# Attention logits on all 128 rows: query halves stacked, key halves written twice

## The chip, the cores and the metric

The kernel runs on one core of one Trainium2 chip. The time is device microseconds of one execution; the number for a kernel is the median of its runs. A core has engines that run side by side, each with a queue of its own: TensorE (PE; its weight loads are listed apart, as PEld), VectorE (DVE), ScalarE (ACT), GpSimd (POOL), and SyncE (SP), which starts transfers. TensorE writes its products to PSUM, eight banks of 128 partitions x 512 float32.

## The reference

One layer of a hybrid block on 512 tokens of width 1024, in float32: RMSNorm; one wide input projection; a gated linear attention branch; a forgetting attention branch (FoX); per-channel sigmoid gates that merge both; an output projection; a gated MLP with a short convolution; a last RMSNorm. The change touches FoX alone:

```python
for i in range(S // Q_BLOCK):                       # 4 blocks of 128 queries
    lo, hi = i * Q_BLOCK, (i + 1) * Q_BLOCK
    logits = jnp.einsum('bhqd,bhkd->bhqk', qh[:, :, lo:hi], kh[:, :, :hi]) * scale
    logits = logits + c[:, :, lo:hi, None] - c[:, :, None, :hi]
    p = softmax(where(mask, logits, -inf))
    outs.append(jnp.einsum('bhqk,bhkd->bhqd', p, vh[:, :, :hi]))
```

There are 8 heads (FH) of width 64 (FD). Query and key are RMS-normalised first.

## The kernel before, in words

TensorE multiplies in a float32 form (`F32R`) that keeps fewer bits. So each operand is split into a high half (a rounded copy, made by ACT) and a low half (what is left, made by DVE), and a product is high x high + high x low + low x high: three matmuls (`mm3`, L323, whose three lines 324 to 326 are most of the profile). Weights come in pieces of 128x1024, loaded by SP, split by ACT (L287) and DVE (L288) three pieces ahead of their use.

The attention loop (L1077) handles two heads, a "pair", at a time: heads 2p and 2p+1 lie on partitions 0-63 and 64-127 of the transposed query and key. For each of four pairs it goes through three groups of query blocks, (0,1), (2) and (3), so 12 steps.

- `prepare_k(pair)` (L936) transposes the pair's key on TensorE (four 128x128 blocks) into a PSUM bank, then ACT copies the high half `kh` (L942) and DVE subtracts the low half `kl` (L943), all 128 partitions at once. `prepare_q` (L947) does so for the query, with a scale per partition (L953, L954). Both kinds of tiles have two buffers.
- `logits(pair, qbs)` (L969): for each query block three products, (qh, kh), (ql, kh), (qh, kl), each once per head, with 64 rows of contraction per head (L979). Then for each head, on DVE, the logits minus their bias with the row maximum (L986), on ACT the exponential with its sum (L991), the reciprocal on DVE and the scaling on ACT (L993). The bias rows `cb` are loaded by SP and masked by POOL (L626 to L628).
- `transposed(h, qbs)` (L1003) transposes the probabilities, and splits them (L1029, L1030); `values(h, half)` (L1034) multiplies them with the value's halves, side by side in one 128-column operand (L1047, L1048).

The steps are software pipelined: in turn i the logits of step i, the transposes of step i-1, the values of step i-2. Between them TensorE works off a list, `work`, by `fill(n)`: n steps of it. Most of the list are gate products (`gate_tile`, L921: 8 steps of three 128x512 matmuls, then one DVE multiplication, L928, that frees the gate's PSUM bank); `prepare_k` and `prepare_q` are in it as steps of their own. The first fills of a turn are put behind the logits on TensorE's queue by hand (`tc.issue_after`, L1079). PSUM in this stage is four kinds of two banks: `mm` (gates, and the transposed query and key), `lg` (logits), `pt`, `po`.

Within these orders the framework's scheduler places the instructions of each engine when the kernel is built: a later instruction that is ready goes ahead of an earlier one that isn't.

Of the kernel before, what the change touches and what calls it, by code (L numbers as in the profile page):

```python
# [9 lines left out]
F32 = mybir.dt.float32  # L10
F32R = mybir.dt.float32r
BF16 = mybir.dt.bfloat16
I32 = mybir.dt.int32
AF = mybir.ActivationFunctionType
ALU = mybir.AluOpType
# [3 lines left out]
P = 128  # L19
T = 512  # L20
# [8 lines left out]
FH, FD = 8, 64  # L29
# [13 lines left out]
QSTEP = 4  # L43
# [41 lines left out]
def hybrid_kernel(ctx: ExitStack, tc, xT, xt, wp, wu, wd, wf, wn, pp, aw2, fing, out):  # L85
    nc = tc.nc
    mm = nc.tensor.matmul
# [16 lines left out]
    def bank(tag):  # L104
        return banks_of[tag].tile([P, 512], F32, tag=tag, name="ps_" + tag)
# [267 lines left out]
    for _ in range(NWARM):  # L373
        mm(  # L374
            warm, lhsT=nc.const_aps.tensor(1.0, (P, P), BF16), rhs=nc.const_aps.tensor(1.0, (P, T), BF16),
            start=True, stop=True,
# [10 lines left out]
    def col(c, rows=P):  # L387
        return ppt[:rows, c : c + 1]
# [5 lines left out]
        out=negm, in_=negm, pattern=[[-1, P]], base=0, channel_multiplier=1, compare_op=ALU.is_ge, fill=-1e30  # L394
# [5 lines left out]
        out=gmask, in_=gmask, pattern=[[1, P]], base=0, channel_multiplier=-1, compare_op=ALU.is_ge, fill=0.0  # L400
# [26 lines left out]
    work = []  # L427

    def fill(n=1 << 30):
        while n > 0 and work:  # L430
            try:
                next(work[0])
                n -= 1
            except StopIteration:
                work.pop(0)
# [75 lines left out]
    for k in range(KD):  # L511
        high = nc.scalar.activation(out=xh[k], in_=xrs[k], func=AF.Copy, scale=col(C_MIX + k))
        split_next()
        with tc.issue_after(first_copy[-1].ins):
            low = nc.vector.scalar_tensor_tensor(
                out=xl[k], in0=xrs[k], scalar=col(C_MIX + k), in1=xh[k].bitcast(F32),
                op0=ALU.mult, op1=ALU.subtract,
# [46 lines left out]
    gqs = cpool.tile([P, 1], F32, name="gqs")  # L564
    with tc.issue_after(low.ins):
        nc.vector.scalar_tensor_tensor(
            out=gqs, in0=col(C_QG), scalar=FD ** -0.5, in1=col(C_KG), op0=ALU.mult, op1=ALU.mult
# [27 lines left out]
    for j in range(2):  # L595
# [4 lines left out]
            out=mz[:, j, :], in0=pz, scalar1=col(C_AB + j), scalar2=0.0, op0=ALU.add, op1=ALU.min  # L600
# [11 lines left out]
        out=bz.rearrange("p a b -> p (a b)"), data0=rmask, data1=mz.rearrange("p a b -> p (a b)"),  # L612
# [4 lines left out]
        out=fm, data0=ones[:FH, 0:1].broadcast_to([FH, T]), data1=ft, initial=0.0, op0=ALU.mult, op1=ALU.add,  # L617
# [183 lines left out]
    for i in range(4):  # L801
        tag = ("ft", "fm", "sc2", "sc3")[i]
# [8 lines left out]
    for tt in range(NT):  # L811
        for j in range(2):
            t = slice(tt * P, (tt + 1) * P)
            c = slice((2 * (tt % 2) + j) * P, (2 * (tt % 2) + j + 1) * P)
            for par in range(2):
                r = slice(par * CH, (par + 1) * CH)
# [9 lines left out]
    def chunk_kv(c, j):  # L826
        i = 2 * (c // 2 % 2) + j
        return pkv[c // 4 * 2 + c % 2][:, i * GDV : (i + 1) * GDV]

    for tt in range(NT):  # L830
        for j in range(2):
            for par in range(2):
                for c in range(2 * tt, min(2 * tt + 2, NC - 1)):
                    r = slice(c % 2 * CH, (c % 2 + 1) * CH)
                    mm(
                        chunk_kv(c, j)[par * CH : (par + 1) * CH],
                        lhsT=kdt[r, tt, j, par * CH : (par + 1) * CH],
                        rhs=vg[r, tt, (2 * j + par) * GDV : (2 * j + par + 1) * GDV],
                        start=True, stop=True,
                    )  # L840
    for tt in range(NT):
        fill(2)
        for c in range(2 * tt, min(2 * tt + 2, NC - 1)):
            for j in range(2):
                if c == 0:
                    last_dve = nc.vector.tensor_copy(out=prev[:, j, 1, :], in_=chunk_kv(c, j))
                else:
                    last_dve = nc.vector.scalar_tensor_tensor(
                        out=prev[:, j, c + 1, :], in0=prev[:, j, c, :], scalar=dec[:, j * NC + c : j * NC + c + 1],
                        in1=chunk_kv(c, j), op0=ALU.mult, op1=ALU.add,  # L850
# [24 lines left out]
    for u in range(2):  # L875
        for par in range(2):
            for t2, j, c in quarters:
# [4 lines left out]
                    rhs=vg[:, 2 * u + t2, h * GDV : (h + 1) * GDV],  # L882
                    start=(t2 == j == 0), stop=False, skip_group_check=True,
                )
    for u in range(2):
        for t2, j, c in quarters:
            for par in range(2):
                r = slice(par * CH, (par + 1) * CH)
                for cp in range(2):
# [3 lines left out]
                        rhs=prev[r, j, ck, :], start=False, stop=True, skip_group_check=True,  # L893
                    )
    for u in range(2):
        for par in range(2):
            for t2, j, c in quarters:
                junk = gpool.tile([P, GDV], F32, tag="gjunk", name="gjunk", bufs=2)
                nc.scalar.activation(
                    out=junk, in_=obs[u][par][:, c], func=AF.Square, accum_out=gssq[:, u, par, t2, j : j + 1]  # L900
# [11 lines left out]
    fpool = es_f.enter_context(tc.tile_pool(name="fpool", bufs=1, reuse_waits="tile"))  # L912
# [8 lines left out]
    def gate_tile(z):  # L921
        ps = pmm()
        wh, wl = piece()
        for k in range(KD):
            c = slice(k * P, (k + 1) * P)
            mm3(ps, wh[:, c], wl[:, c], xh[k], xl[k], k == 0, k == KD - 1)
            yield
        nc.vector.tensor_mul(out=z, in0=ps, in1=rb)  # L928

    gates = [gate_tile(z) for z in zr + zg]  # L930


    psum(mm=2, lg=2, pt=2, po=2)
    qk, vs = {}, {}

    def prepare_k(pair):  # L936

        pk = bank("mm" if pair else "po")
        for tt in range(NT):
            nc.tensor.transpose(pk[:, tt * P : (tt + 1) * P], kf[:, tt, pair * P : (pair + 1) * P], ident)  # L940
        kh, kl = (fpool.tile([P, T], F32R, tag=tag, name=tag, bufs=2) for tag in ("kh", "kl"))
        nc.scalar.copy(out=kh, in_=pk)  # L942
        nc.vector.tensor_sub(out=kl, in0=pk, in1=kh.bitcast(F32))  # L943
        qk[pair] = [kh, kl]
        yield

    def prepare_q(pair):  # L947

        pq = bank("mm" if pair else "pt")
        for tt in range(NT):  # L950
            nc.tensor.transpose(pq[:, tt * P : (tt + 1) * P], qf[:, tt, pair * P : (pair + 1) * P], ident)
        qh, ql = (fpool.tile([P, T], F32R, tag=tag, name=tag, bufs=2) for tag in ("qh", "ql"))
        nc.scalar.activation(out=qh, in_=pq, func=AF.Copy, scale=gqs)  # L953
        nc.vector.scalar_tensor_tensor(  # L954
            out=ql, in0=pq, scalar=gqs, in1=qh.bitcast(F32), op0=ALU.mult, op1=ALU.subtract
        )
        qk[pair] += [qh, ql]
        yield

    def prepare_v(h):  # L960
# [7 lines left out]

    def logits(pair, qbs):  # L969

        kh, kl, qh, ql = qk[pair]
        rows = [slice(i * FD, (i + 1) * FD) for i in range(2)]
        lgs = [bank("lg") for _ in range(2)]
        for qb in qbs:
            n = (qb + 1) * P
            q = slice(qb * P, n)
            for j, (a, b) in enumerate(((qh, kh), (ql, kh), (qh, kl))):
                for lg, r in zip(lgs, rows):
                    last = mm(lg[:, place_of_q(qb)], lhsT=a[r, q], rhs=b[r, :n], start=(j == 0), stop=(j == 2))  # L979
        for i, lg in enumerate(lgs):  # L980
            h = 2 * pair + i
            pr = probs[h, qbs] = fpool.tile([P, T], F32, tag="pr", name="pr", bufs=4)
            for qb in qbs:
                p = pr[:, place_of_q(qb)]
                nm = fpool.tile([P, 1], F32, tag="nm", name="nm", bufs=4)
                nc.vector.tensor_tensor_reduce(  # L986
                    out=p, in0=lg[:, place_of_q(qb)], in1=cbs.pop((h, qb)), scale=-1.0, scalar=3e38,
                    op0=ALU.add, op1=ALU.min, accum_out=nm,
                )
                rs = fpool.tile([P, 1], F32, tag="rs", name="rs", bufs=4)  # L990
                nc.scalar.activation(out=p, in_=p, func=AF.Exp, scale=-1.0, bias=nm, accum_out=rs)  # L991
                nc.vector.reciprocal(out=rs, in_=rs)
                nc.scalar.activation(out=p, in_=p, func=AF.Copy, scale=rs)  # L993
                if h + 2 < FH:
                    load_cb(h + 2, qb)
        return last

    def place_of_q(qb):

        a = P if qb == 1 else 0  # L1000
        return slice(a, a + (qb + 1) * P)
# [62 lines left out]
        nc.vector.tensor_sub(out=otl[pair], in0=oo[pair], in1=oth[pair].bitcast(F32))  # L1064

    steps_a = [(pair, qbs) for pair in range(FH // 2) for qbs in QBS]
    work += [islice(gates[0], 4), prepare_k(0), prepare_q(0), gates[0]]
    work += [islice(gates[1], QSTEP), prepare_k(1), gates[1], islice(gates[2], QSTEP), prepare_q(1), gates[2]]
    for pair in range(2, FH // 2):
        work += [prepare_k(pair), gates[2 * pair - 1], prepare_q(pair), gates[2 * pair]]  # L1070
    work += gates[FH - 1 :]
    fill(6)
    for h in range(2):
        prepare_v(h)
    fill(3)
    NG = len(QBS)
    for i in range(len(steps_a) + 2):  # L1077
        if i < len(steps_a):
            with tc.issue_after(logits(*steps_a[i]).ins):  # L1079
                fill(FILL[i % NG][0])  # L1080
        for j in range(2):
            if 0 <= i - 1 < len(steps_a):
                transposed(2 * steps_a[i - 1][0] + j, steps_a[i - 1][1])
                fill(FILL[i % NG][1 + j])
        if i >= 2 and steps_a[i - 2][1][-1] % 2 == 1:
            pair, qbs = steps_a[i - 2]
            for j in range(2):
                values(2 * pair + j, qbs[-1] // 2)

        if i > NG and i % NG == 2:  # L1090
            split_values(i // NG - 1)
# [41 lines left out]
    for h in range(GH):  # L1133
# [4 lines left out]
            out=zr[h], in0=ogr[h], scalar=col(C_OG + h), in1=zr[h], op0=ALU.mult, op1=ALU.mult  # L1138
# [178 lines left out]
    for g in range(2):  # L1317
        n = at_step[g, 5]
# [87 lines left out]
    def halves(x):  # L1406
        return x.rearrange("p (i t) -> p i t", t=H)
# [84 lines left out]
    for n, (g, p) in enumerate(steps):  # L1492
# [4 lines left out]
        name = {1: "x", 2: "x", 5: "z", 3: "z", 6: "y", 7: "y", 4: "y"}[p]  # L1497
# [16 lines left out]
        elif p == 4:  # L1514
# [5 lines left out]
            for i, c in enumerate((st["x"], ps)):  # L1520
                for j, k, fs in parts:
                    nc.vector.tensor_mul(
                        out=act[j][:, i, k], in0=halves(c)[:, fs], in1=t0[:, fs, i * H : (i + 1) * H]
# [147 lines left out]
    last = [piece() for _ in range(NTAIL)]  # L1671
# [109 lines left out]
```

## Time and profile before

| | |
|---|---|
| median of 3 runs | 696.99 us (696.96 to 697.45) |
| profiled execution | 697.62 us |
| its span, first to last instruction | 695.9 us |
| granted TensorE clock | 0.998 |
| attention loop | from 132 to 217 us of the span |
| logits matmuls | 96: 32 for each of the three products |

A row of the instruction view is: start, duration, engine, line, operation, output tile <- input tiles, shape, count, and in brackets the idle time before it and what ended that. "64*128" is a matmul on 64 rows with 128 output columns of weights, "64x512" what streams through it. Durations of matmuls overlap, since the engine is a pipeline: from start to start is what one costs. The rows of the stretches give the length and then the busy time of each engine in it. In the chain of waits a piece runs from the end of the one before it to its own end.

### The profile page before, as it was taken

Reading aid. Unit: us, or ns where it says so; the run is one execution under the profiler, and the core shown is the slowest. Engines: PE = TensorE matmul, PEld = TensorE weight load, DVE = VectorE, ACT = ScalarE, POOL = GpSimd, SP = SyncE. Lnnn points to the kernel's source line nnn. Section 1 sums busy time; section 2 is a strip of 40 time slices with the busy share of each in tenths; the row PEclk is TensorE's granted clock in tenths of the full one; section 3 lists DMA queues with packets and bytes.
Section 4 is the critical chain, followed back from the end, with each engine's and each line's share of the span. In section 5 each row is a group of like instructions: output and inputs, shape, how many; then the busy total and the mean of one; then the engine's idle time right before and its main releaser. Section 6 shows DMA issues by size and latency. Waiting matters only on the chain.

```text
span 695.9 us, 11191 instructions
## 1 busy us (share of the span) xinstructions
PE 688.8 (99%) x4163; PEld 600.1 (86%) x4163; DVE 546.4 (79%) x823; ACT 426.5 (61%) x688; POOL 170.2 (24%) x220
## 2 busy tenths in 40 slices
PE   9999999999999999999999999999999999999996
PEld 6788888787878888888888999999999999888886
DVE  6774989766675676587679998888998889977984
ACT  7487776677666844344583866565556556655753
POOL 1125010134231324332110134423433311000222
PEclk9999999999999999999999999999999999999999
DMA  8769498887665389967975777877777788866643
GB/s 305 272 191 308 87 281 231 282 240 163 161 157 135 79 248 206 257 159 211 223 244 131 164 168 197 210 163 180 176 188 175 184 208 248 270 197 178 196 137 122
DMA packets 45035, 138.08 MB, mean 198 GB/s; under 512 B 5268, under 2 KB 9260, under 8 KB 44852
## 3 DMA queue, kind: packets, MB, share of 16 engines
q1 hardware_dynamic: 31156, 92.98, 39.8%
q0 software_dynamic: 10656, 39.33, 31.8%
q10 hardware_dynamic: 3168, 5.05, 2.0%
q8 instruction: 33, 0.54, 0.3%
q14 instruction: 22, 0.18, 0.1%
HBM read 133.13 MB, written 27.28 MB: 230 GB/s over the span
## 4 chain that ended last, share of the span: by engine, by line
PE 93%; DVE 4%; DMA 1%; ACT 1%; issue 1%; DVEq 0%; SPq 0%; ACTq 0%
PE ps_mm L324 21%; PE ps_mm L325 21%; PE ps_mm L326 21%; PE ps_ax L325 7%; PE ps_ax L326 7%; PE ps_ax L324 7%; DVE wl L288 1%; PE ps_lg L979 1%; PE ps_pt L1013 1%; DMA rawx<-wsum 1%; PE ps_mm L485 1%; PE ps_po L1048 1%; PE ps_po L1047 1%; PE ps_ax L374 1%; DVE xo L1346 1%
## 5 line engine op out<-in xcount | busy, mean ns | idle before, releaser
L287 ACT CAST wh<-rawx 128x1024 fp32r<-128x1024 f32 x75 | 76.2, 1016 | 52.9 <-PE ps_mm L325 18.9
L324 PE MATMUL ps_mm<-xh,wh 128*128 128x512 f32 (+1 forms) x304 | 106.2, 349 | 0.2 <-DVE zg L928 0.2
L325 PE MATMUL ps_mm<-xl,wh 128*128 128x512 f32 (+1 forms) x304 | 103.3, 340 | 0.0
L326 PE MATMUL ps_mm<-xh,wl 128*128 128x512 f32 (+1 forms) x304 | 103.2, 340 | 0.0
L288 DVE TENSOR_TENSOR wl<-rawx,wh 128x1024 fp32r<-128x1024 f32 x75 | 90.0, 1203 | 16.0 <-ACT wh L287 15.9
L288 DVE TENSOR_TENSOR wl<-raw,wh 128x1024 fp32r<-128x1024 f32 x58 | 77.1, 1331 | 9.5 <-ACT wh L287 9.2
L287 ACT CAST wh<-raw 128x1024 fp32r<-128x1024 f32 x58 | 60.7, 1049 | 35.7 <-PE ps_mm L325 30.5
L324 PEld LDWEIGHTS ps_mm<-xh,wh 128*128 128x128 f32 x304 | 57.7, 190 | 9.3 <-issue 1.8
L326 PEld LDWEIGHTS ps_mm<-xh,wl 128*128 128x128 f32 x304 | 57.7, 190 | 6.7
L325 PEld LDWEIGHTS ps_mm<-xl,wh 128*128 128x128 f32 x304 | 57.8, 190 | 5.5 <-DVE xl L1255 0.2
L295 POOL DMA_DIRECT2D rawx<-in_wu_dram x30 | 26.1, 871 | 123.8 <-DVE wl L288 118.8
L288 DVE TENSOR_TENSOR wl<-rawz,wh 128x1024 fp32r<-128x1024 f32 x31 | 39.5, 1274 | 14.9 <-ACT wh L287 14.7
L324 PE MATMUL ps_mm<-xo,wh 128*128 128x256 f32 x160 | 45.4, 284 | 0.0
L326 PE MATMUL ps_mm<-xo,wl 128*128 128x256 f32 x160 | 45.3, 283 | 0.0
L325 PE MATMUL ps_mm<-xo,wh 128*128 128x256 f32 x160 | 45.3, 283 | 0.0
L324 PE MATMUL ps_mm<-xc,wh 128*128 128x256 f32 (+1 forms) x128 | 43.4, 339 | 0.0
L258 POOL TENSOR_TENSOR rawx<-rawx,raw 128x256 f32<-128x256 f32 x32 | 37.2, 1189 | 22.7 <-DMA rawx<-in_wu_dram 22.7
L325 PE MATMUL ps_mm<-xc,wh 128*128 128x256 f32 (+1 forms) x128 | 42.3, 331 | 0.0
L326 PE MATMUL ps_mm<-xc,wl 128*128 128x256 f32 (+1 forms) x128 | 42.3, 331 | 0.0
L1399 DVE SCALAR_TENSOR_TENSOR t<-ap,ppt,t 128x512 f32<-128x512 f32 x44 | 40.9, 984 | 0.0
L287 ACT CAST wh<-rawz 128x1024 fp32r<-128x1024 f32 x31 | 32.4, 1045 | 13.2 <-issue 5.1
L324 PE MATMUL ps_mm<-wh,xh 128*128 128x512 f32 x96 | 37.7, 392 | 0.0
(495 smaller groups left out, 1987.6 us busy)
## 6 DMA issues: line engine op xcount, KB each, us to landing
rawx<-in_wu_dram POOLq DMA_DIRECT2D x32, 512.0 KB, 6.1
rawz<-in_wp_dram SPq DMA_DIRECT2D x30, 512.0 KB, 5.6
raw<-in_wp_dram SPq DMA_DIRECT2D x22, 512.0 KB, 4.7
wsum<-in_wd_dram SPq DMA_DIRECT2D x20, 512.0 KB, 6.8
rawx<-in_wu_dram SPq DMA_DIRECT2D x20, 512.0 KB, 5.5
raw<-in_wu_dram SPq DMA_DIRECT2D x20, 512.0 KB, 4.7
rawx<-wsum SPq DMA_DIRECT2D x12, 512.0 KB, 4.5
wsum<-in_wd_dram POOLq DMA_DIRECT2D x10, 512.0 KB, 8.3
```

What stands on the lines that cost most here:

```text
L258: nc.gpsimd.tensor_add(out=raws[n][:, c], in0=raws[n][:, c], in1=raws[other][:, c])
L287: nc.scalar.copy(out=hi[:, :m], in_=raw[:, :m])
L288: nc.vector.tensor_sub(out=lo[:, :m], in0=raw[:, :m], in1=hi[:, :m].bitcast(F32))
L295: added[:] = [nc.gpsimd.dma_start(raw, recipes[i][0], accum_op=ALU.add)]
L324: mm(ps, lhsT=ah, rhs=bh, start=start, stop=False, **k)
L325: mm(ps, lhsT=ah, rhs=bl, start=False, stop=False, **k)
L326: mm(ps, lhsT=al, rhs=bh, start=False, stop=stop, **k)
L374: mm(warm, lhsT=nc.const_aps.tensor(1.0, (P, P), BF16), rhs=nc.const_aps.tensor(1.0, (P, T), BF16), start=True, stop=True,)
L485: mm(first[i], lhsT=w[:, i * P : (i + 1) * P], rhs=x, start=(k == j == 0), stop=False)
L979: last = mm(lg[:, place_of_q(qb)], lhsT=a[r, q], rhs=b[r, :n], start=(j == 0), stop=(j == 2))
L1013: nc.tensor.transpose(pt[:, len(parts) * P : (len(parts) + 1) * P], pr[:, c : c + P], ident)
L1399: nc.vector.scalar_tensor_tensor(out=t0[:, i], in0=ap[:, i, w : w + T], scalar=col(C_CW + w * NF + f), in1=t0[:, i], op0=ALU.mult, op1=ALU ...
```

## The change

For a head the high query lies on its own 64 partitions and its low query on the other 64, in one tile `q2[:, i]`; the key's high half is written to both halves of the partitions, and so is its low half (`kh[:, i]`, `kl[:, i]`). One matmul of 128 rows then gives (high + low query) x high key, a second one (high + low query) x low key. The product low x low, which was left out before, is in it.

```diff
     def prepare_k(pair):
...
-        kh, kl = (fpool.tile([P, T], F32R, tag=tag, name=tag, bufs=2) for tag in ("kh", "kl"))
-        nc.scalar.copy(out=kh, in_=pk)
-        nc.vector.tensor_sub(out=kl, in0=pk, in1=kh.bitcast(F32))
-        qk[pair] = [kh, kl]
-        yield
+        kh, kl = (fpool.tile([P, 2, T], F32R, tag=tag, name=tag) for tag in ("kh", "kl"))
+        for i, r in enumerate(HEADS):
+            nc.scalar.copy(out=kh[r, i], in_=pk[r])
+            nc.scalar.copy(out=kh[HEADS[1 - i], i], in_=pk[r])
+        for i, r in enumerate(HEADS):
+            for out in HEADS:
+                nc.vector.tensor_sub(out=kl[out, i], in0=pk[r], in1=kh[r, i].bitcast(F32))
+        ks[pair] = kh, kl
     def prepare_q(pair):
...
+        q2 = qs[pair] = fpool.tile([P, 2, T], F32R, tag="q2", name="q2", bufs=2)
+        for i, r in enumerate(HEADS):
+            nc.scalar.activation(out=q2[r, i], in_=pq[r], func=AF.Copy, scale=gqs[r])
+            nc.vector.scalar_tensor_tensor(
+                out=q2[HEADS[1 - i], i], in0=pq[r], scalar=gqs[r], in1=q2[r, i].bitcast(F32),
+                op0=ALU.mult, op1=ALU.subtract,
+            )
     def logits(pair, qbs):
-        for qb in qbs:
-            n = (qb + 1) * P
-            q = slice(qb * P, n)
-            for j, (a, b) in enumerate(((qh, kh), (ql, kh), (qh, kl))):
-                for lg, r in zip(lgs, rows):
-                    last = mm(lg[:, place_of_q(qb)], lhsT=a[r, q], rhs=b[r, :n], start=(j == 0), stop=(j == 2))
+        for i, lg in enumerate(lgs):
+            for qb in qbs:
+                n = (qb + 1) * P
+                for j, k2 in enumerate(ks[pair]):
+                    last = mm(
+                        lg[:, place_of_q(qb)], lhsT=qs[pair][:, i, qb * P : n], rhs=k2[:, i, :n], start=(j == 0),
+                        stop=(j == 1),
+                    )
...
-    work += [islice(gates[0], 4), prepare_k(0), prepare_q(0), gates[0]]
-    work += [islice(gates[1], QSTEP), prepare_k(1), gates[1], islice(gates[2], QSTEP), prepare_q(1), gates[2]]
+    work += [islice(gates[0], 4), prepare_q(0), gates[0], islice(gates[1], QSTEP), prepare_q(1), gates[1], gates[2]]
     for pair in range(2, FH // 2):
-        work += [prepare_k(pair), gates[2 * pair - 1], prepare_q(pair), gates[2 * pair]]
+        work += [gates[2 * pair - 1], prepare_q(pair), gates[2 * pair]]
     work += gates[FH - 1 :]
-    fill(6)
+    fill(4)
+    prepare_k(0)
+    fill(1)
...
             with tc.issue_after(logits(*steps_a[i]).ins):
+                if i % NG == NG - 1 and i + 1 < len(steps_a):
+                    prepare_k(steps_a[i + 1][0])
                 fill(FILL[i % NG][0])
```

The key's tiles are twice as wide and have one buffer (no `bufs=2`), the query's tile is twice as wide with two buffers; the memory they take is the same. `prepare_k` is no longer a step of the list: it is called directly, for the first pair ahead of the loop, for the others behind the last logits of the pair before. `HEADS` are the two halves of the partitions.

More of the change, by code (lines that the diff above doesn't have):

```diff
@@ L933, in hybrid_kernel @@
     psum(mm=2, lg=2, pt=2, po=2)
-    qk, vs = {}, {}
+    qs, ks, vs = {}, {}, {}
+    HEADS = [slice(i * FD, (i + 1) * FD) for i in range(2)]
     def prepare_k(pair):
@@ L951, in prepare_q @@
             nc.tensor.transpose(pq[:, tt * P : (tt + 1) * P], qf[:, tt, pair * P : (pair + 1) * P], ident)
[L952 to L957, printed above, removed]
+        q2 = qs[pair] = fpool.tile([P, 2, T], F32R, tag="q2", name="q2", bufs=2)
[5 more added lines that the diff above has]
+            )
         yield
@@ L969, in logits @@
     def logits(pair, qbs):
-        kh, kl, qh, ql = qk[pair]
-        rows = [slice(i * FD, (i + 1) * FD) for i in range(2)]
         lgs = [bank("lg") for _ in range(2)]
-        for qb in qbs:
-            n = (qb + 1) * P
-            q = slice(qb * P, n)
-            for j, (a, b) in enumerate(((qh, kh), (ql, kh), (qh, kl))):
-                for lg, r in zip(lgs, rows):
-                    last = mm(lg[:, place_of_q(qb)], lhsT=a[r, q], rhs=b[r, :n], start=(j == 0), stop=(j == 2))
+        for i, lg in enumerate(lgs):
[6 more added lines that the diff above has]
+                    )
         for i, lg in enumerate(lgs):
```

## The prediction

> **What bounds the kernel now.** I read the page first, then the busy time of the engines in the stage where the logits are made, then that stage instruction by instruction on TensorE, then the chain of waits there.
>
> ```profile
> span 695.9 us, 11191 instructions
> ...
> PE 688.8 (99%) x4163; PEld 600.1 (86%) x4163; DVE 546.4 (79%) x823; ACT 426.5 (61%) x688; POOL 170.2 (24%) x220
> ...
> PE 93%; DVE 4%; DMA 1%; ACT 1%; issue 1%; DVEq 0%; SPq 0%; ACTq 0%
> ```
>
> TensorE is busy all through and 93% of the chain that ends last is its own work. The attention loop lies from 132 to 217 us; the row of that stretch gives, after its length, the busy time of PE, PEld, DVE, ACT and POOL:
>
> ```profile
> 132.00:217.00 85.00, 84.84 (x493) 67.97 (x492) 56.80 (x144) 59.08 (x140) 26.33 (x51) 1.00 0.76 184
> ```
>
> Of 85.00 us TensorE misses 0.16. What the change takes from TensorE here comes off the end, and so does any wait it puts there. DVE is 67% and ACT 70% busy: each has room on average, but not in every stretch. The first logits step on TensorE (start, duration; x2 is the two heads, which start together):
>
> ```profile
> 132.09 0.39 PE L326 MATMUL ps_mm<-xc,wl 128*128 128x512 f32 x1
> 132.41 0.33 PE L979 MATMUL ps_lg<-kh,qh 64*128 64x128 f32 x2
> 132.57 0.28 PE L979 MATMUL ps_lg<-kh,ql 64*128 64x128 f32 x2
> ...
> 133.09 0.28 PE L979 MATMUL ps_lg<-kl,qh 64*128 64x256 f32 x2
> 133.30 0.50 PE L324 MATMUL ps_mm<-xc,wh 128*128 128x512 f32 x1
> 133.64 0.39 PE L325 MATMUL ps_mm<-xc,wh 128*128 128x512 f32 x1
> ```
>
> Two things stand in it. The two heads use half the rows each and run side by side, so twelve matmuls take the time of six. And there is a toll around them: 0.32 us from the last gate matmul to the first logit, and 0.34 us from the first gate matmul behind to the second, where gate matmuls otherwise start 0.23 apart. The chain of waits gives the step as ends, start and length of each piece:
>
> ```profile
> 132.48 0.89 PE ps_lg L979 x12
> 133.37 0.43 PE ps_mm L324
> 133.80 0.23 PE ps_mm L325
> ...
> 135.64 0.72 PE ps_lg L979 x6
> 136.36 0.43 PE ps_mm L324
> ...
> 142.50 0.89 PE ps_lg L979 x6
> 143.40 0.43 PE ps_mm L324
> ```
>
> A step costs its own piece plus what the next gate matmul has over 0.23: 0.89 + 0.20 = 1.09 us for query blocks 0 and 1, 0.92 for block 2, 1.09 for block 3. That is 3.10 us a head pair and 12.4 us for four.
>
> **The change, TensorE.** Each head and block now has two matmuls on all 128 rows, with nothing side by side: four slots where there were three, and 64 matmuls for 96. No run shows logits in that form. The nearest row is the products with the values, which are 128-row matmuls in the same number format; eight of them, four of 256 columns and four of 128, are just what the new step of blocks 0 and 1 has:
>
> ```profile
> 222.85 0.39 PE L326 MATMUL ps_mm<-xh,wl 128*128 128x512 f32 x1
> 223.08 0.28 PE L1047 MATMUL ps_po<-ph,v 128*128 128x256 f32 x1
> ...
> 223.84 0.27 PE L1048 MATMUL ps_po<-pl,v 128*128 128x128 f32 x1
> 223.95 0.62 PE L1013 MATMUL ps_pt<-ident,pr 128*128 128x128 f32 x4
> ```
>
> From the first to the next thing on the engine are 0.87 us, and ahead of them stands the usual 0.23 and no gap. Behind, I allow 0.07 of the 0.11 that the gate matmul at 133.30 has over 0.23. So 0.94 against 1.09. Block 3 is four matmuls of 512 columns at 0.23, 0.92 against 1.09. Block 2 lies between by its columns: 384/512 of 0.23 is 0.17, four are 0.69, with 0.02 behind 0.71 against 0.92. Saved: 0.15 + 0.17 + 0.21 = 0.53 a pair, 2.1 for four; I take **-2.0**. Its bounds are -2.3 (nothing behind the short ones) and, if the toll stays although the rows are full, a loss: one product more per block, 0.11 + 0.12 + 0.17 + 0.23 = 0.63 a pair, +2.5 in all.
>
> The Trainium skill speaks on both sides here. "TensorEngine Tiling (Array Packing)", section When to Use Tiling, asks for two-fold row tiling when the contraction is 64 or less, which is the form that is given up; by that alone the sum would be the +2.5 above. The same page, Key Properties, says that changing the tiling mode drains the engine; the 0.32 and 0.34 above agree with it, and by it the toll goes when all matmuls have 128 rows. I follow the second, because the values' rows show no such gap.
>
> **The change, ACT and DVE.** The copies and subtractions now go by halves of the partitions. The row of a 64-partition copy and add beside those of 128 partitions:
>
> ```profile
> L942 ACT CAST kh<-ps_mm x3: 561/568/589, 140.2 to 170.8; 128x512 fp32r<-128x512 f32 x3
> L943 DVE TENSOR_TENSOR kl<-ps_mm,kh x3: 687/692/692, 140.8 to 171.4; 128x512 fp32r<-128x512 f32 x3
> L953 ACT ACTIVATE qh<-ps_mm,gqs x3: 668/674/685, 147.8 to 179.9; 128x512 fp32r<-128x512 f32 x3
> L954 DVE SCALAR_TENSOR_TENSOR ql<-ps_mm,gqs,qh x3: 750/751/751, 148.5 to 180.6; 128x512 fp32r<-128x512 f32 x3
> L1057 ACT COPY ol<-ps_po x8: 583/585/588, 165.6 to 231.2; 64x512 f32<-64x512 f32 x8
> L1058 DVE TENSOR_TENSOR oo<-ps_po,ol x8: 683/683/684, 166.2 to 232.1; 64x512 f32<-64x512 f32 x8
> ```
>
> Half the partitions take the same time (585 ns against 568, 683 against 692). So a pair's key costs four copies (2.3 us) and four subtractions (2.8) where it had one of each, and its query two and two. Added per pair: ACT 3 x 0.57 + 0.67 = 2.4, DVE 3 x 0.69 + 0.75 = 2.8; in all 9.5 and 11.3 us. Against 26 and 28 us of idle time in the loop this fits on average and costs nothing by itself. It costs where TensorE waits for its end, at four places.
>
> *The first pair.* Its key is the last thing ready before the loop:
>
> ```profile
> 130.03 0.38 PE L940 MATMUL ps_po<-ident,kf 128*128 128x128 f32 x2
> ...
> 130.45 0.59 ACT L942 CAST kh<-ps_po 128x512 fp32r<-128x512 f32 x1 [0.81 <-PE ps_po L940]
> ...
> 130.05 0.74 DVE L954 SCALAR_TENSOR_TENSOR ql<-ps_pt,gqs,qh 128x512 fp32r<-128x512 f32 x1
> 131.07 0.69 DVE L943 TENSOR_TENSOR kl<-ps_po,kh 128x512 fp32r<-128x512 f32 x1 [0.28 <-ACT kh L942]
> ```
>
> Now: subtraction done at 131.76, logits at 132.41, so 0.65 us to spare. After: DVE has two query subtractions from 130.05, to 131.5, and then four key subtractions, two of them behind the third copy (130.45 + three copies of some 0.5 = 132.0). The second ends near 132.9, the fourth near 134.1. Head 0's matmuls wait from 132.3 to 132.9 and run 0.45; head 1's wait until 134.1. That is 0.6 + 0.75, some **+1.2**, since the gate matmuls behind are queued behind these logits by the kernel's own order. Bounds 0.5 (the key goes ahead of the query on DVE) and 1.8.
>
> *The three changes of pair.* The key tiles have one buffer now, so the key of the next pair is made between the last logits of one and the first of the next. The copies' wait for the old key's readers costs nothing: the transposes are queued behind those logits. Behind the copies on ACT wait the casts of probabilities and weights, behind the subtractions on DVE the gate products and probabilities' low halves. The three stretches, from those last logits to the end of the next:
>
> ```profile
> 142.40:151.20 8.80, 8.80 (x58) 7.17 (x57) 6.36 (x13) 5.38 (x11) 4.92 (x10) 1.00 0.91 234
> 166.40:175.70 9.30, 9.14 (x59) 7.31 (x58) 6.76 (x14) 6.63 (x14) 4.32 (x7) 1.00 0.59 119
> 191.20:200.20 9.00, 9.00 (x57) 7.27 (x56) 7.00 (x13) 6.21 (x13) 4.03 (x6) 1.00 0.67 152
> ```
>
> DVE is idle 2.44, 2.54 and 2.00 us. It gets four subtractions in each, 2.77; from the first goes one query subtraction (0.75 at 148.5; it is step 14 of the list now and was step 24), the second holds one key subtraction already (0.69). So 2.02, 2.08 and 2.77 come in: just covered twice, 0.77 over the third time. ACT gets some 1.7, 1.7 and 2.3 on idle 3.42, 2.67 and 2.79. Some of the idle time cannot be used, and a second thing waits: the key's PSUM bank is one of the two that the gates use, held until its last subtraction. TensorE's one stall in the loop is of that sort already:
>
> ```profile
> 168.83 0.60 PE L940 MATMUL ps_mm<-ident,kf 128*128 128x128 f32 x4
> ...
> 170.49 0.50 PE L324 MATMUL ps_mm<-xh,wh 128*128 128x512 f32 x1 [0.16 <-DVE zg L928]
> ```
>
> Against that, a weight subtraction of 1.22 us can slip behind. I take 0.3 a change, **+0.9**; bounds 0 and 1.5 each (the second rival).
>
> *The end of the loop.* The key no longer counts as a step of filler, so of four gate steps that lay in the last turn of the loop one is left: behind the last transposes TensorE has 0.7 us less to do, and 1.4 less ahead of them.
>
> ```profile
> 226.66 0.44 PE ps_pt L1013 x4
> ...
> 227.75 0.69 DVE L1030 TENSOR_TENSOR pl<-ps_pt,ph 128x512 fp32r<-128x512 f32 x1 [1.83 <-ACT ph L1029]
> ```
>
> From the transposes' end, 227.1, to the low half's, 228.44, are 1.3 us, which 0.94 us of the other head's values cover in part. **+0.2**, between 0 (the next gates are pulled ahead) and 0.6.
>
> The moved query brings no new operation but the second copy and subtraction; the loads of the bias rows and the writes behind them keep their place, and neither SP's nor POOL's queue is passed.
>
> Sum: -2.0 + 1.2 + 0.9 + 0.2 = +0.3. The profiled execution took 697.62 (1.72 outside its span) and gives 697.9; the median of the runs, 696.99, lies 0.6 under it, so the forecast in their terms is 697.3. What is won or lost here should pass on whole, as TensorE has no gap to swallow it until the last stretch.
>
> **Rivals.** *All hidden.* The key's four copies start in ACT's idle time ahead of the exponentials, and the first logits are reached late enough. Then the 2.0 stay: 695.0, or 695.6 with half of the start's wait. For it: the 56.80 of 85.00. Against: 0.65 us to spare at the start for 2.3 us of added chain. 25%.
>
> *ACT's and DVE's chain decides at each change of pair: slower.* If the copies stand behind the softmax, as the last pair's key, at 170.8, stood behind most of it:
>
> ```profile
> 146.20 1.33 ACT L993 ACTIVATE pr<-pr,rs 128x512 f32<-128x512 f32 x2
> ...
> 150.34 0.33 PE L979 MATMUL ps_lg<-kh,qh 64*128 64x128 f32 x2
> ```
>
> The softmax ends at 147.5, the first copy at 148.1, and four subtractions from there at 150.9, or 151.6 with one low half of 0.69 between them. The logits, without their toll, want the last at 150.1. It decides once the fourth subtraction ends over 7 us after the last pair's logits. 0.8 to 1.5 late, three times: 2.4 to 4.5 in place of 0.9, so 698.8 to 700.9. 24%.
>
> *The packing was worth more than its toll.* The gaps belong to short matmuls, not to the rows, and stay: +2.5 in place of -2.0, and 701.8 with the rest of the sum, 699.5 if all waits vanish. The Trainium skill's When to Use Tiling points here. Against it stand the values' rows, which are as short and have no gap. 8%.
>
> **How the numbers follow.** The smallest change that a measurement of this kernel tells from none is about 0.2%, 1.4 us. The forecast (43%, own range 695.6 to 698.4) is within it: same 0.43. Faster is the first rival, 0.25. Slower is the other two, 0.32. The range, 694.9 to 700.2, holds the forecast, the first rival and the lower part of the slower two; below is left some 5%, above some 13%.
>
> **What would show it.** Right: logits as 128x128 matmuls with no 0.32 us ahead and no 0.34 behind; some 10.3 us in all for the steps on TensorE in place of 12.4; a wait of the first logits for the key's low half near 1.2 us; short waits of gates or logits for DVE at the three changes. Wrong: those gaps still there; logits waiting 1 us and more for the key at each change; DVE busy under 65 us in the loop; or no wait at all before the first logits.

## The result and the profile after

| | before | after |
|---|---|---|
| median, same chip | 697.22 us (4 runs) | 707.32 us (4 runs, 707.14 to 707.58) |
| ratio | | 1.0141 [1.0129, 1.0154] |
| profiled execution, its span | 697.62, 695.9 us | 707.37, 705.7 us |
| granted TensorE clock, whole span | 0.998 | 0.995 |

The change costs 10 us, 1.4%, well above the range. The page of the kernel after, the lines that answer to those of before:

```profile
PE 691.9 (98%) x4131; PEld 604.8 (86%) x4131; DVE 555.9 (79%) x839; ACT 436.4 (62%) x704; POOL 170.9 (24%) x220
...
PE 83%; DVE 6%; issue 4%; ACT 4%; DMA 2%; POOL 0%; DVEq 0%; ACTq 0%; POOLq 0%
```

DVE and ACT have some 10 us more work each. But TensorE's share of the chain fell from 93% to 83%: now other engines set the pace somewhere. Where, the stretches of the kernel after show (length, then busy time of PE, PEld, DVE, ACT and POOL, then the granted clock):

```profile
132.40:137.30 4.90, 2.45 (x8) 1.87 (x9) 3.40 (x8) 1.66 (x6) 0.00 (x0) 0.74 0.92 247
137.30:140.80 3.50, 3.50 (x11) 2.73 (x10) 1.54 (x8) 2.86 (x11) 0.43 (x1) 0.50 0.29 81
...
132.00:217.00 85.00, 79.55 (x413) 66.04 (x413) 59.74 (x148) 62.41 (x141) 22.34 (x46) 0.96 0.64 160
```

Of the attention loop's 85 us TensorE misses 5.45 where it missed 0.16, and 2.45 of them lie in the first 5 us, at the first logits. A second loss does not show in the busy time: from 137.3 to 140.8 us TensorE is all busy, but at a clock of 0.50. The half clock starts earlier, while TensorE still waits, and lasts some 6.8 us:

```profile
131.30:134.70 3.40, 1.44 (x6) 0.69 (x4) 1.75 (x3) 2.27 (x4) 0.67 (x1) 1.00 1.00 339
134.70:141.50 6.80, 5.99 (x17) 4.83 (x18) 3.90 (x15) 4.00 (x12) 0.57 (x2) 0.50 0.49 116
```

To see how much is lost up to the end of the loop, one needs a point at which both kernels have done the same work. The first matmul on `ogh`, behind the loop, is one: ahead of it stand the same matmuls in both, but for the logits. It starts at 254.22 us, against 245.85 before, so 8.4 of the 9.8 us by which the span grew are lost up to there.

The waits of TensorE, in the kernel after, name who was late (total us, times, longest):

```profile
PE ps_lg L982 <- DVE kl L949: 2.9, 4, 1.1
PE ps_lg L982 <- ACT kh L946: 1.3, 2, 0.9
...
PE ps_ax L326 <- DVE wl L288: 0.6, 1, 0.6
PE ps_mm L325 <- DVE ogl L1151: 0.6, 1, 0.6
PE ps_mm L324 <- DVE kl L949: 0.5, 1, 0.5
...
PE ps_mm L324 <- DVE zg L928: 0.3, 1, 0.3
```

The key's low half `kl` and the second copies of its high half (L946) lead. None of these stood among the waits of before except the last, with 0.2. The two of 0.6 lie behind the loop, near 407 and at 256.6 us. The chain of waits through the first logits, in the kernel after (start, length, piece):

```profile
131.25 0.58 ACT kh L945
...
131.84 0.58 ACT kh L946
...
132.44 0.58 ACT kh L945
...
133.04 0.59 ACT kh L946
...
133.65 0.68 DVE kl L949
...
134.35 0.68 DVE kl L949
...
135.06 0.69 DVE kl L949
...
135.77 0.70 DVE kl L949
...
136.52 1.01 PE ps_lg L982 x3
137.53 0.43 PE ps_mm L324
137.95 0.43 PE ps_mm L325
```

This is the picture of the loss: four copies one behind the other, then four subtractions one behind the other, no subtraction beside a copy, and TensorE at the end of it. The last two pieces are gate matmuls, each 0.43. The first took as long before, with its toll, but the second took 0.23: that is the half clock. The instruction view says the same of DVE and ACT there, with one wait more, that of the second query copy:

```profile
130.54 0.68 ACT L959 ACTIVATE q<-ps_pt,gqs 64x512 fp32r<-64x512 f32 x1 [1.30 <-DVE q L960]
131.26 0.75 DVE L960 SCALAR_TENSOR_TENSOR q<-ps_pt,gqs,q 64x512 fp32r<-64x512 f32 x1 [0.75 <-ACT q L959]
133.65 2.81 DVE L949 TENSOR_TENSOR kl<-ps_po,kh 64x512 fp32r<-64x512 f32 x4 [1.64 <-ACT kh L946]
```

DVE had nothing to do for 1.64 us, although head 0's first copy, the only one that its first two subtractions need by their data, was done at 131.83.

### The profile page after: what moved, and what is told of

It is laid out like the page before. It is cut to its first block, busy times and chain, and to the rows that moved or that the text cites. A ratio compares the mean times of both kernels' runs of the same rounds, so it can differ in the third digit from the quotient of the medians.

```text
span 705.7 us, 11175 instructions
## 1 busy us (share of the span) xinstructions
PE 691.9 (98%) x4131; PEld 604.8 (86%) x4131; DVE 555.9 (79%) x839; ACT 436.4 (62%) x704; POOL 170.9 (24%) x220
## 4 chain that ended last, share of the span: by engine, by line
PE 83%; DVE 6%; issue 4%; ACT 4%; DMA 2%; POOL 0%; DVEq 0%; ACTq 0%; POOLq 0%
PE ps_mm L324 19%; PE ps_mm L325 19%; PE ps_mm L326 19%; PE ps_ax L326 7%; PE ps_ax L325 7%; PE ps_ax L324 7%; DVE wl L288 2%; DMA rawx<-in_wu_dram 1%; PE ps_lg L982 1%; DVE kl L949 1%; PE ps_mm L485 1%; PE ps_pt L1019 1%; ACT wh L287 1%; DMA ppt<-in_pp_dram 1%; DVE ogl L1151 1%
## 5 line engine op out<-in xcount | busy, mean ns | idle before, releaser
L288 DVE TENSOR_TENSOR wl<-raw,wh 128x1024 fp32r<-128x1024 f32 x58 | 75.3, 1299 | 8.6 <-ACT wh L287 8.3
L1408 DVE SCALAR_TENSOR_TENSOR t<-ap,ppt,t 128x512 f32<-128x512 f32 x44 | 42.4, 1016 | 0.0
```

The source lines that it names most:

```text
L288: nc.vector.tensor_sub(out=lo[:, :m], in0=raw[:, :m], in1=hi[:, :m].bitcast(F32))
L1408: nc.vector.scalar_tensor_tensor(out=t0[:, i], in0=ap[:, i, w : w + T], scalar=col(C_CW + w * NF + f), in1=t0[:, i], op0=ALU.mult, op1=ALU ...
```

## The experiments

The theory from these rows: TensorE's part of the change is a gain as forecast, and the loss is the order of the preparation. A copy on ACT and a subtraction on DVE that read the same PSUM bank are kept in program order, whether or not their data has to do with each other. (Each bank is one PSUM tile of the program here, so no run tells apart whether the order goes by the tile or by the bank; "bank" below means either.) Rivals: the full-row matmuls themselves are slower; the order comes from the shared SBUF tiles and not from the bank; the added work fills DVE; the change in the order of filler and key is what costs. Ratios are against the kernel before on the same chip, with a 95% interval.

**The new matmuls alone.** The kernel before with its own preparation, and only the 64 matmuls of 128 rows in place of the 96:

```diff
-                for j, (a, b) in enumerate(((qh, kh), (ql, kh), (qh, kl))):
-                    for lg, r in zip(lgs, rows): mm(... lhsT=a[r, q], rhs=b[r, :n] ...)
+        for lg in lgs:
+            for qb in qbs:
+                for j, (a, b) in enumerate(((qh, kh), (ql, kl))): mm(... lhsT=a[:, q], rhs=b[:, :n] ...)
```

> The kernel before with its own preparation of query and key, and only the logits' matmuls in the new form: per head and block two of 128 rows, (high query, high key) and (low query, low key), each over both heads' rows at once. The sums are not the logits; nothing else is left out. Theory A (TensorE waits longer for operands that now take four copies and four subtractions, and the matmuls themselves gain): 694.9 to 695.7, 1.5 to 2.3 under the kernel before, no gap ahead of the logits and none behind. Theory B (giving up the side-by-side heads costs on TensorE): 699 to 702.

Measured: 695.68 us, 0.9973 [0.9962, 0.9984]. The chain of waits of this kernel:

```profile
133.08 0.92 PE ps_lg L979 x8
134.00 0.23 PE ps_mm L324
...
136.05 0.71 PE ps_lg L979 x4
136.75 0.24 PE ps_mm L324
...
142.71 0.91 PE ps_lg L979 x4
143.62 0.23 PE ps_mm L324
```

The gate matmul behind each step takes 0.23, where it took 0.43 before: the toll is gone. The steps cost 0.92, 0.71 and 0.91, where the prediction had 0.94, 0.71 and 0.92. The saving of 1.8 us fits the forecast -2.0. The matmuls are no part of the loss.

**The new preparation alone.** The kernel after, with the old pattern of three 64-row products per head and block, reading the new tiles:

```diff
-                for j, k2 in enumerate(ks[pair]): mm(... lhsT=qs[pair][:, i, q], rhs=k2[:, i, :n] ...)
+            for j, k2 in enumerate((kh, kh, kl)):
+                for i, lg in enumerate(lgs):
+                    r = HEADS[1 - i]
+                    mm(... lhsT=qs[pair][r, i, q], rhs=k2[r, i, :n] ...)
```

> The changed kernel with its new preparation, and the logits' matmuls in the old form: 64 rows, two heads side by side, three per block, all on the half of the partitions that the second writes fill. The operands of the products are not the right ones; the count, shape and waits are those of the old form. Theory A: the loss is all here, 708 to 710, with the first logits waiting some 4 us and the gates behind them at half the clock. Theory B: near the kernel before, 697 to 699.

Measured: 710.48 us, 1.0183 [1.0162, 1.0205]. The preparation alone is slower than before by 13.0 us, and slower than the kernel after by about 3. So the two parts of the change have opposite signs, and the whole loss is in the preparation. They do not add up exactly, 13.0 - 1.8 = 11.2 against 10.1; in the profile of this run the clock is at 0.50 in two places, for 3.4 and 6.8 us, against one of 6.8 in the kernel after.

**A tile of its own for each head.** If the order comes from two heads sharing a tile, it goes when `q2`, `kh` and `kl` are separate tiles (the diff shows the key's):

```diff
-        kh, kl = (fpool.tile([P, 2, T], F32R, tag=tag, name=tag) for tag in ("kh", "kl"))
+        kh, kl = ([fpool.tile([P, T], F32R, tag=f"{tag}{i}", name=tag) for i in range(2)] for tag in ("kh", "kl"))
```

> The changed kernel with a tile of its own for each head's stacked query, high key and low key; same instructions in the same order. If the subtractions of the key wait for all four copies, and the second copy of the query for the first subtraction, because they write one tile: both waits go, some 2.5 us at the first pair and 1 at each change of pair, 702 to 704. If they wait because ACT and DVE read the same PSUM bank: unchanged, 706.5 to 708.

Measured: 706.91 us, 1.0136 [1.0121, 1.0151], as the kernel after. ACT and DVE in this kernel:

```profile
130.56 0.68 ACT L959 ACTIVATE q<-ps_pt,gqs 64x512 fp32r<-64x512 f32 x1 [1.30 <-DVE q L960]
...
133.67 2.81 DVE L949 TENSOR_TENSOR kl<-ps_po,kh 64x512 fp32r<-64x512 f32 x4 [1.64 <-ACT kh L946]
```

The same wait for the same fourth copy, although the first two subtractions now share no SBUF tile with it, and not even partitions of the bank. The second query copy waits for the first query subtraction as before, too. The rival falls.

**Leaving the bank sooner.** The second copies read the first ones in SBUF instead of the bank, and the query's two copies stand ahead of its two subtractions. The number of instructions stays the same:

```diff
         for i, r in enumerate(HEADS):
             nc.scalar.copy(out=kh[r, i], in_=pk[r])
-            nc.scalar.copy(out=kh[HEADS[1 - i], i], in_=pk[r])
+        for i, r in enumerate(HEADS):
+            nc.scalar.copy(out=kh[HEADS[1 - i], i], in_=kh[r, i].bitcast(F32))
...
             nc.scalar.activation(out=q2[r, i], in_=pq[r], func=AF.Copy, scale=gqs[r])
+        for i, r in enumerate(HEADS):
             nc.vector.scalar_tensor_tensor(
```

> The changed kernel; the second copies of the high key read the first ones in SBUF in place of the PSUM bank, and both copies of the query come ahead of both subtractions. If the order of ACT's and DVE's reads of one PSUM bank makes the waits: the key's subtractions wait for two copies in place of four (1.2 us sooner each time), the query's second copy for nothing (1.3 us at the first pair), so 702 to 705. If the tile makes them: the subtractions still wait for the last copy, 706 to 707.5. If it is the sheer work on DVE and ACT: unchanged, 707.

Measured: 700.09 us, 1.0038 [1.0024, 1.0053]: 7.2 of the 10.1 us are back. The same place in this kernel, instruction by instruction:

```profile
129.73 1.53 DVE L962 SCALAR_TENSOR_TENSOR q<-ps_pt,gqs,q 64x512 fp32r<-64x512 f32 x2
...
130.07 1.18 ACT L945 CAST kh<-ps_po 64x512 fp32r<-64x512 f32 x2
...
131.16 1.26 ACT L947 CAST kh<-kh 64x512 fp32r<-64x512 f32 x2
...
131.29 2.81 DVE L950 TENSOR_TENSOR kl<-ps_po,kh 64x512 fp32r<-64x512 f32 x4
```

The query's subtractions follow each other without a wait. The key's start right behind them, at 131.29, and run beside the two copies that read SBUF, though these stand ahead of them in the program. Whether they still wait for both copies that read the bank can't be read off here, since those ended just before (131.25) and DVE was busy until then. It can at the change to the third pair:

```profile
171.38 1.19 ACT L945 CAST kh<-ps_mm 64x512 fp32r<-64x512 f32 x2
...
172.60 2.10 DVE L950 TENSOR_TENSOR kl<-ps_mm,kh 64x512 fp32r<-64x512 f32 x3 [0.57 <-ACT kh L945]
```

DVE idles 0.57 us, the length of one copy, until the other head's copy out of the bank has ended, at 172.57. So the order in the bank is still there, only with less in it. The clock at the first logits is whole:

```profile
132.40:137.30 4.90, 4.01 (x20) 3.39 (x21) 3.83 (x16) 2.86 (x13) 0.16 (x1) 1.00 0.92 261
```

How much of the 7.2 belongs to the key and how much to the query was not tried apart.

**Keeping TensorE busy during the wait.** The kernel after with 18 matmuls of constants (128x512, bf16) ahead of the first logits, into a bank that the first logits then overwrite:

```diff
+        if pair == 0 and qbs == QBS[0]:
+            for _ in range(18):
+                mm(lgs[0], lhsT=nc.const_aps.tensor(1.0, (P, P), BF16), rhs=nc.const_aps.tensor(1.0, (P, T), BF16),
+                   start=True, stop=True)
```

> The changed kernel with 18 matmuls of constant ones put ahead of the first logits, into a bank that the logits then overwrite: 4.1 us of work that counts for nothing, in the place where TensorE waits for the first pair's operands. If the half clock behind that wait (nine gate matmuls at 0.43 us in place of 0.23, and the first logits of the next step) is a result of the wait: 1.8 to 2.2 us come back, 705.1 to 705.6, and the gates stand at 0.23. If the clock falls for another reason, or the idle time was not the cause: 707 to 708.

Measured: 705.31 us, 1.0112 [1.0097, 1.0127], so 2.0 us less than the kernel after. The two stretches in this kernel:

```profile
132.40:137.30 4.90, 4.90 (x27) 2.92 (x26) 3.35 (x9) 1.48 (x4) 0.00 (x0) 1.00 0.92 247
137.30:140.80 3.50, 3.50 (x18) 2.99 (x17) 2.68 (x15) 3.50 (x13) 0.00 (x0) 1.00 0.28 69
```

The key's low half is ready no sooner than it was, but TensorE is busy in the wait and keeps its clock, with 18 matmuls from 137.3 to 140.8 in place of 11. So some 2 us of the loss are the half clock, a consequence of the first wait.

**What is left of the order: six runs on the version that leaves the bank sooner (700.09 us).** More gates ahead of the first logits, `fill(3)` to `fill(6)`:

> On the version that leaves the PSUM bank sooner (700.1): three gate steps more, 2.1 us, are taken from the list ahead of the first logits. If the wait at the first pair (LG takes 2.7 us in place of 0.9 there) is latency that other work can cover: 1.5 to 1.8 less, 698.3 to 698.7, less what the end of the loop loses with three steps less of filler (0 to 1.5). If DVE's and ACT's work is the limit, nothing is won: 700.

Measured: 700.11 us, 1.0036 [1.0023, 1.0049]. The first wait goes and the time does not. TensorE's waits in this kernel:

```profile
PE ps_mm L957 <- DVE kl L950: 0.8, 1, 0.8
...
PE ps_mm L324 <- DVE q L962: 0.5, 1, 0.5
...
PE ps_mm L324 <- DVE kl L950: 0.4, 1, 0.4
```

None is for the logits' operands. In these three the tiles on the left are `ps_mm`, the two banks that the gates use: what is late is the bank that a preparation holds until its last subtraction. Work put ahead of the first wait only moved the wait.

Less work on DVE: the second low halves as SBUF copies, 423 ns in place of 688.

```diff
+            nc.vector.tensor_sub(out=kl[r, i], in0=pk[r], in1=kh[r, i].bitcast(F32))
+        for i, r in enumerate(HEADS):
+            nc.vector.tensor_copy(out=kl[HEADS[1 - i], i], in_=kl[r, i].bitcast(F32))
```

> On the version that leaves the PSUM bank sooner (700.1): the second copies of the key's low half are plain copies in SBUF on DVE in place of subtractions from PSUM. If the work on DVE limits, a copy in SBUF that takes under 0.69 us shows: at 0.35 us it takes 0.7 us off each chain, 698 to 699.5. If the waits left are the order of the banks and the fill, it stays at 699.8 to 700.3.

Measured: 700.53 us, 1.0037 [1.0025, 1.0050]. DVE's busy time in the loop window went from 63.79 to 62.01 and nothing was won: DVE's volume is not what binds.

Both together:

> The last two together, three gate steps more ahead of the loop and the low halves copied. If the loss is the operands' latency and nothing else, 697 to 698.5, about the kernel before; the matmuls alone would allow 695.7.

Measured: 699.50 us, 1.0028 [1.0018, 1.0039], which its interval does not tell from either alone.

The key always in a bank of kind `po`, none of which the gates use, and nothing else:

```diff
-        pk = bank("mm" if pair else "po")
+        pk = bank("po")
```

> The version that leaves the PSUM bank sooner (700.1) with only the key's bank changed, from the gates' to the values'. If the gates' waits at the changes of pair (gaps of 0.4 to 0.6 us, three or four) come from the bank that the key holds: 0.8 to 1.6 less, 698.5 to 699.3. If not: 699.8 to 700.4.

Measured: 699.05 us, 1.0022 [1.0012, 1.0032]. With the key in `mm`, two waits of gates for a bank that an earlier gate holds until its multiplication stand among TensorE's waits:

```profile
PE ps_mm L324 <- DVE zg L928: 0.3, 1, 0.3
...
PE ps_mm L324 <- DVE zr L928: 0.2, 1, 0.2
```

With the key in `po` neither is there. The medians differ by about 1 us, more than these two waits, and that is at the edge of what the intervals tell apart.

That edit on top of both others, with the query's preparation moved to the first step of a gate, and the same with four gate steps first in place of six:

> The last version (699.5) with the transposed key always in a bank of the values' accumulators, which are free at that point, in place of one of the gates' two, and the query's preparation moved to the first step of a gate. If the waits that are left (1.3, 0.6 and 0.5 us of gates for DVE) are the gates' missing second bank: 1.5 to 2.5 us less, 697 to 698. If they are DVE's and ACT's work or the order of the loop: 699 to 700.

> The first of these three with one gate step more ahead of the loop in place of three. If the end of the loop lacks what is taken from it to the front, this is 0.5 to 1 better than the first; if the first pair's wait decides, 0.5 to 1 worse.

Measured: 699.10 us, 1.0027 [1.0018, 1.0036], and 699.07 us, 1.0022 [1.0013, 1.0031]. The bank alone gives as much as all of these together.

**The first pair and the filler, on the version with the key in `po` (699.05 us).** One gate step less in each third turn, so that more filler is left for the end of the loop, `(3, 3, 2)` to `(3, 3, 1)`:

> On the version with the key's bank changed (699.05): one gate step less in the last turn of each pair, where the key's transposes now stand, so that four are left for the end of the loop, as before the change. If the waits of 0.5 and 1.0 us at and behind the loop's end are a lack of filler: 698.0 to 698.5. If they are not: 699.

Measured: 700.62 us, 1.0039 [1.0025, 1.0054]. Not better. The wait for `ogl` behind the loop is gone, but two new ones come up, the longer because a gate's multiplication stands behind four row maxima on DVE. TensorE in this kernel, first the row of the longer wait:

```profile
180.74 0.50 PE L324 MATMUL ps_mm<-xh,wh 128*128 128x512 f32 x1 [1.79 <-DVE zg L928]
```

The other stands in the list of waits (POOL makes the value's low half `v`):

```profile
PE ps_po L1055 <- POOL v L972: 0.9, 1, 0.9
```

The first pair prepared and multiplied in the old form, the other three in the new one (the diff shows the key's part; the query's and the logits' are alike):

```diff
+        if pair == 0:
+            nc.scalar.copy(out=kh[:, 0], in_=pk)
+            nc.vector.tensor_sub(out=kl[:, 0], in0=pk, in1=kh[:, 0].bitcast(F32))
+            return
```

> On the version with the key's bank changed (699.05): the first pair alone is prepared and multiplied in the old form (one copy and one subtraction each, 64 rows, two heads side by side). If the first logits' wait for their operands (gaps of 0.57 and 1.10 us in place of 0.11 each) is what is lost there: 1.4 us less by the wait, 0.5 more by the old matmuls, 698.0 to 698.4. If the wait only moves on to the next stage of the same pair: 698.8 to 699.5.

Measured: 698.22 us, 1.0010 [1.0001, 1.0018]: the best of all versions, level with the kernel before by the 0.2% of the prediction, and not faster. TensorE's waits in it:

```profile
PE ps_mm L324 <- DVE q L974: 0.8, 2, 0.5
PE ps_mm L325 <- DVE ogl L1175: 0.6, 1, 0.6
```

No wait for the key is left. The longest in the loop is that of a gate for the query's bank:

```profile
143.43 0.47 PE L324 MATMUL ps_mm<-xh,wh 128*128 128x512 f32 x1 [0.53 <-DVE q L974]
```

Both edits in one kernel:

> On the version with the key's bank changed (699.05): the next two edits together. If the rest of the loss is the first pair's wait (1.3 us over what its matmuls gain) and the filler missing at the loop's end (1 to 1.4 us): 696.4 to 697.2, under the kernel before. If it is spread over the changes of pair: 698 to 699.

Measured: 699.78 us, 1.0037 [1.0022, 1.0051], with single runs from 697.65 to 705.07. The wait of 1.79 us at 180.9 is there too, and in its profile the clock falls behind it:

```profile
182.05:185.45 3.40, 3.40 (x11) 2.63 (x10) 1.68 (x3) 3.34 (x6) 0.78 (x2) 0.50 0.42 115
```

So filler kept back in this way does not win the rest.

## Why the prediction was wrong, step by step

- **TensorE, -2.0: right.** The steps and the toll came out as worked out, -1.8 alone. The rival that the packing is worth more than its toll is refuted by the first experiment, and with it, for this kernel, the advice of the Trainium skill, "TensorEngine Tiling (Array Packing)", section When to Use Tiling, to row-tile a contraction of 64 two-fold.
- **ACT's and DVE's volume: right.** Half the partitions took 0.58 us on ACT and 0.69 on DVE, as the rows of 64 partitions said, and the page's totals grew by 9.9 us (ACT) and 9.5 (DVE), against 9.5 and 11.3. DVE's busy time under 65 us in the loop, named as a sign of the contrary, did show (59.74), but only because the loop grew and less of it lies in the window.
- **The first pair, +1.2 within 0.5 to 1.8: the step that failed.** It let two subtractions run "behind the third copy" while the fourth was still to come. In fact all four waited for the fourth, the copies began 0.8 us later because the second query copy waited for the first query subtraction, and they lay 0.60 apart, not 0.5. (The sum also came out 0.2 short by its own prices: four subtractions of 0.69 from 131.5 end at 134.3, not 134.1.) The last gate matmul ahead starts at 131.70, so the next thing could start at 131.93; the next gate starts at 137.32. These are 5.39 us for a step of 0.94: 4.45 lost, against 1.2. Some 0.4 of them are the half clock: from gate to gate, start to start, it is 5.62 us here and 5.26 with the wait filled. The prices of the instructions were near; what may run beside what was taken from the data alone, not from the bank that both engines read. The two runs on tiles and bank show the cause: the order stays with separate tiles, and goes for those copies that no longer read the bank.
- **Not in the sum at all: the clock.** Nine gate matmuls at 0.43 in place of 0.23 are 1.8 us; filling the wait gave back 2.0.
- **The three changes of pair, +0.9: too small.** TensorE's distances there, less the 0.23 or so that belong to them, are 0.67 and 0.55 at pair 1, 0.75, 0.32 and 0.29 at pair 2, and 0.38 at pair 3: 3.0 in all. The first three, 2.0, wait for the key's low half; the others for row maxima and a gate's multiplication that come late on DVE. That is the second rival's 2.4 to 4.5, and by its mechanism, copies behind the softmax. The kernel after, at pair 1:

```profile
153.52 1.32 ACT L999 ACTIVATE pr<-pr,rs 128x512 f32<-128x512 f32 x2
154.75 0.57 ACT L946 CAST kh<-ps_mm 64x512 fp32r<-64x512 f32 x1
...
155.35 2.81 DVE L949 TENSOR_TENSOR kl<-ps_mm,kh 64x512 fp32r<-64x512 f32 x4 [1.54 <-ACT kh L946]
...
156.78 0.33 PE L982 MATMUL ps_lg<-kl,q 128*128 128x128 f32 x1 [0.63 <-DVE kl L949]
...
158.31 0.47 PE L324 MATMUL ps_mm<-xh,wh 128*128 128x512 f32 x1 [0.51 <-DVE kl L949]
```

The softmax slipped in ahead of the fourth copy only, but since all four subtractions wait for that one, it delays them all. First the logits wait, then a gate for the bank. So the same order in the bank made this term large too.
- **The end of the loop, +0.2: about 1.** 0.3 at 235 us, and 0.8 at 255.60, where the low half `ogl` of a gated output comes late. Whether the missing filler makes that one was not tried apart.
- **Balance.** -1.8 + 4.45 + 1.8 + 3.0 + 1.1 = 8.5 of the 9.8 us. Of the other 1.3, 0.6 are the wait for a weight's low half near 407 us, and 0.2 the second logits step, which in part still ran at half clock (from 141.16 to 142.04, 0.88 in place of 0.71). The rest was not traced.

What stays open: with the order, the key's bank and the first pair mended, 698.22 is still 2.5 us above what the matmuls alone reach (695.68). In that profile there are small waits for the query's preparation (0.8) and for `ogl` (0.6), and the toll in the first pair's old steps; more filler ahead, less DVE work and filler kept back did not win it. A second buffer for the key's tiles was not tried. Nor was the changed order of filler and key, the last of the rivals, run by itself: with it in place 7.2 of the 10.1 us came back, so it can account for no more than a part of the rest.

## What to carry to other kernels

Ask of two instructions on different engines not only whether one needs the other's data, but whether both touch one PSUM bank: if so, write them so that the bank is read as few times as possible, with the copies ahead of the subtractions, and make further copies from SBUF. A gain on the engine that bounds the kernel is small beside one exposed chain on the others, so lay out the whole chain in front of the first use, instruction behind instruction, in its worst order, and take that as the bound. And look at the granted clock behind a wait of TensorE: here the half clock cost some 2 us on top of the wait itself.

## What the runs showed of the hardware that was not expected

- The half clock came without a long gap. It began at 134.7 us and lasted some 6.8 us. In the 3.4 us ahead of it TensorE was busy for 1.44, and the longest distance from one matmul's start to the next around it was 1.41 us. Where TensorE was busy for 4.01 of 4.90 us, in the version that leaves the bank sooner, the clock stayed whole. The Trainium skill, "TensorE: Matmul & The Clock Gate", Part 1, has the clock fall after an idle window of some 3.4 us that runs freely. The lengths agree with that, 6.8 us being twice 3.4 and the half clock with both edits at the end of the experiments 3.4, but here the clock fell behind 3.4 us that were not idle. After the wait of 1.79 us the clock fell in one profile (both edits) and stayed at 1.00 in the other (the filler alone), so the same gap may or may not cost it.
- Reads by ACT and DVE of one bank were kept in order even where they lay on different partitions: the first two subtractions read partitions 0 to 63, the two copies that they waited for 64 to 127. The Trainium skill, "PSUM — Partial Sum Buffer", section PSUM bank collisions raise a hardware error, says that two engines must not touch the same bank and 32-partition quadrant at once, and may share a bank in different quadrants. By it only a part of the order seen here is asked for; no run shows whether the rest could be left out.
- The toll between matmuls of 64 and of 128 rows was worth more than the fourth slot that the full-row form takes: 1.8 us over twelve steps.
